# Four seams of a hybrid recurrent step: two hidden tiles' plain products first, operands in token halves, residual rows on GpSimd's DMA queue

## The chip, the cores and the metric

The kernel runs on one core of one Trainium2 chip. The metric is the device time of one execution in microseconds. Before the change three runs gave 2541.56, 2547.58 and 2551.4 us; the median is 2547.58 us.

## The reference, cut to what matters

One inference step of a two-layer trunk over 1048 columns (16 meta tokens and 1024 prompt tokens of one sequence, then 8 samples of one token each), in float32. Layer 0 is a mixer of gated linear attention and an S5 state space; layer 1 is a Griffin block (convolution, RG-LRU). After each mixer comes the same gated ConvFFN, and its two ends are what the change touches:

```
def conv_ffn(x, buf, norm, w_up, conv_w, conv_b, w_down):
    hup = rmsnorm(x, norm) @ w_up                     # 1024 -> 2 x 2816
    gate, val = jnp.split(hup, 2, axis=-1)
    gate, new_buf = causal_dwconv(gate, buf, conv_w, conv_b)   # width 3
    return x + (jax.nn.gelu(gate) * val) @ w_down, new_buf     # 2816 -> 1024

def trunk(x, ...):
    for layer in range(DEPTH):
        if layer % 2 == 0: x, ... = even_mixer(x, ...)   # x + mix @ w_out_0
        else:              x, ... = odd_mixer(x, ...)    # x + y @ w_out_1
        x, nb = conv_ffn(x, buf_ffn[layer], ...)
    return rmsnorm(x, norm_final), ...
```

## The kernel before, in words

Everything lies transposed: 128 channels on the partitions, T tokens in the free dimension (1048 columns; HALF is 524), so the residual is eight tiles X 0 to 7 of 128 x T. A float32 product is made of three fp32r matmuls (`mm3`, L123 to L130): high part by high, low by high, high by low. `split` (L84) makes the parts: a cast on ScalarE (L85) and a subtraction on VectorE (L45, the helper that records every `tensor_tensor`; L48 records the fused `scalar_tensor_tensor`). Weights come by SyncE's DMA queue in tiles of 128 x 512 (`load_w`) and are split in the same way.

The up projection (`ffn_up`) runs over 22 tiles of hidden channels (`hidden(t)`). Each needs a gate and a value for both token halves, a 2 x 2 block product in (gate, value) and (input channels) by (token halves), which is made with seven products (Strassen's scheme in Winograd's form) in the order B11, B21, T2, T3, T1, B22, T4. A product is 4 column tiles x 3 parts x 2 chunks of 262 columns, that is 24 matmuls. B11, B21 and B22 are plain: their operand is a gained half of X, their weight a block as it is. T1 to T4 have sums: of X halves on one side (`Seven.sums`, for a pair of column tiles j and j + 4, so four chains of them), of weight blocks on the other (`sums(t)` in `ffn_up`, on GpSimd, into the tiles wS from wA). All operands are split into high and low, `o[op, j]`. The output hdr[t] goes to memory.

The operands are built where the new residual comes to be. For layer 0 that is the loop after the mixer (i from 0 to 7 over X tiles, the last product of w_out0, L1027 to L1048): PE makes two products, VectorE adds them to x, ScalarE squares and GpSimd adds up the squares (`stats`, the tile acc), x is stored to xdn[m] by SyncE, the plain operand is split off, and after every second tile follow the sums. For layer 1 it is `out(*steps_[-1], prev)` with `after` (L1471 to L1479): the Griffin block runs over token halves and four groups G, and the last of these steps completes X. Its eight B11 and B21 operands are split just ahead of that call; they need only the first token half. The column sum over the partitions is a matmul with a tile of ones (`colsum`, L147) into a PSUM bank, and the inverse norm RB is made from it (`rinv_from`). It scales the products afterwards, so products can start before it is there.

At the head of `ffn_up` the convolution's cache FC is loaded on ScalarE's queue and GpSimd makes the cached terms `pre` from it. Then hidden(0) asks for its weights, the weight sums and the products in the order above.

The down projection (`ffn_down`) first loads X 0 to 7 back from xdn on SyncE's queue (L1174), then goes in turns over hidden tiles: first tiles 0 and 1, then five turns of four. For each tile of a turn hr is loaded from hdr[t] (L1180, two buffers) and split into ph and pl (six buffers each). Each of the eight output tiles then takes k x 3 matmuls a chunk of 352 columns into one of four banks and an addition to X[m]. In layer 0 the last turn also makes the operands of the Griffin block (`Next.step`: HL, X with its gain, split), in layer 1 the final norm.

The order of the work: the framework takes the instructions in the order of the program, with `tc.high_priority()` and `tc.issue_after()` moving some, and lays them out on the engines by a simulated time; on the chip each engine and each DMA queue is in order. Tiles live in pools that are opened at the left or the right end of SBUF; a tile placed where an older one lay waits for that one's last reader (`reuse_waits="tile"`), which is how a load at a seam can be held by the work of the stage before.

Of the kernel before, what the change touches and what calls it, by code (L numbers as in the profile page):

```python
# [9 lines left out]
F32 = mybir.dt.float32  # L10
# [29 lines left out]
def hybrid_step_kernel(ctx: ExitStack, tc: tile.TileContext, a: dict):  # L40
# [896 lines left out]
    NEG = cst.tile([128, 16], F32, name="NEG")  # L937
    ts(NEG, CV[:, CV_GF0:CV_GF0 + 16], -1.0, MUL)
# [5 lines left out]
    class Stats:  # L944
# [5 lines left out]
        def finish(self, before=None):  # L950

            while self.late and (before is None or self.late[0][0] <= before):
                _, c0, n = self.late.pop(0)
                rinv_from(self.acc[c0], n, RB[:, c0:c0 + n])
# [12 lines left out]

    class Next(Stats):


        def __init__(self, gain, pool):
            super().__init__()
            self.gain = gain
            self.HL = [new_hl(pool, k) for k in range(8)]

        def step(self, m, x, c0, n):
            self.n_ += 1
            self.finish(self.n_ - LATE)
            split_gain(self.HL[m][0][:, c0:c0 + n], self.HL[m][1][:, c0:c0 + n], x, self.gain + m)
# [4 lines left out]
    class Seven(Stats):  # L984


        def __init__(self, layer, pool, stats=None):
            super().__init__()
            if stats:
                self.acc, self.late, self.n_ = stats.acc, stats.late, stats.n_  # L990
            self.gain, self.ng = CV_GF0 + 8 * layer, 8 * layer
            self.o = {}
            for j in range(4):
                self.new(j, OPS if j < 3 else OPS[:2] + OPS[5:6], pool)

        def new(self, j, ops, pool):
            for k in ops:
                self.o[k, j] = tuple(pool.tile([128, HALF], F32R, name=f"{k}{j}{x}") for x in "hl")
# [6 lines left out]
        def sums(self, j, x1, x2, pool):  # L1005

            g1, g2 = (CV[:, self.gain + m:self.gain + m + 1] for m in (j, j + 4))
            n1 = NEG[:, self.ng + j:self.ng + j + 1]
# [14 lines left out]

    bms, bm = open_pool("bm0", "right")
    xts, xt = open_pool("xt0", "right")
    nx = Seven(0, bm)
    for i in range(8):  # L1027
# [11 lines left out]
        nc.sync.dma_start(out=xdn[m], in_=x)  # L1039
        nx.plain(j, x, "B21" if i % 2 else "B11")  # L1040
        if m == 7:
            l0.close()
            bls, bl = open_pool("bl0")
            nx.new(3, OPS[2:5] + OPS[6:], bl)
# [10 lines left out]
    def ffn_up(layer, nx):  # L1055
# [11 lines left out]
        wv = CV[:, CV_FC + layer * 4 * NFF:CV_FC + (layer + 1) * 4 * NFF].rearrange("p (j t) -> p j t", j=4)  # L1067

        def wb(j):
            return wv[:, j].unsqueeze(2).to_broadcast([128, NFF, 8])  # L1070

        pt = fp.tile([128, NFF, 8], F32, name="pt")
        tt(pre, FC[:, :, 0], wb(0), MUL, P)
        tt(pre, pre, wb(3), ADD, P)
        tt(pt, FC[:, :, 1], wb(1), MUL, P)
        tt(pre, pre, pt, ADD, P)
        P.tensor_copy(out=FC[:, :, 0], in_=FC[:, :, 1])
# [7 lines left out]
        def sums(t):  # L1085

            r = {}
            for i, k in ((1, 0), (1, 1), (0, 0), (0, 1)):
                r[i, k] = fp.tile([128, 512], F32, name="wA", bufs=4)
                nc.sync.dma_start(out=r[i, k], in_=block(t, i, k))  # L1090
            s1, s2, s3, s4_ = (fp.tile([128, 512], F32, name="wS", bufs=3) for _ in range(4))
# [12 lines left out]
        def hidden(t):  # L1104
            w11, w12 = plain(t, 0, 0), plain(t, 0, 1)
            ws2, ws3, ws1, ws4 = sums(t)
            w22 = plain(t, 1, 1)
            R = fp.tile([128, 2 + T], F32, name="R", tag="rvc", bufs=5)
            VL = fp.tile([128, T], F32, name="VL", tag="rvc", bufs=5)
            P.memset(R[:, 0:2], 0.0)  # L1110
            Z = [bank() for _ in range(2)]
            W, Y = ([ps.tile([128, 512], F32, name="p", tag="aux", bufs=4) for _ in range(2)] for _ in range(2))
# [561 lines left out]
```

## Time and profile before

| | |
|---|---|
| median of three runs | 2547.58 us (2541.56 to 2551.4) |
| profiled execution | 2545.16 us, span 2542.5 us |
| PE busy | 2369.5 us, 93% (17427 matmuls) |
| VectorE (DVE) busy | 1797.4 us, 71% |
| ScalarE (ACT) busy | 1116.6 us, 44% |
| GpSimd (POOL) busy | 556.5 us, 22% |

Times in the rows are microseconds from the start of the span unless marked ns. PE is TensorE's matmul, PEld its weight load; SPq is SyncE's DMA queue and ACTq ScalarE's. `out<-in` names the tiles of the program, `L128` the line of the kernel. In square brackets stands the idle time ahead of an instruction and what ended it.

The stages of this execution: layer 0's mixer to 476; the loop that completes its residual to 525; up projection to 990; down projection 1011 to 1226; the Griffin block to 1748; its last step with the operands of the second up projection to 1801; up projection to 2251; down projection and final norm 2272 to 2543. The seams are the places between them.

### The profile page before, as it was taken

To read this page: it belongs to the slowest core of one execution; us is meant where nothing else is said; L and a number is where in the kernel's file an instruction comes from. 1 tells how busy PE (TensorE), PEld (TensorE's weight loads), DVE (VectorE), ACT (ScalarE), POOL (GpSimd) and SP (SyncE) were. 2 spreads that over 40 slices of the span, in tenths; PEclk is the share of its full clock that TensorE was granted. 3 is DMA by queue.
4 is the path that set the end of the run, shared out by engine and by line. 5 is a ranking of instruction groups with operands and counts; after the bars stand their busy time and mean duration, and the time that the engine had idled before them with its cause. 6 is when DMAs were issued, how large, how long until landed. Compare 5 with 4: busy or idle time off the path is not lost. (4 is left out here: it accounts for less than half of the span.)

```text
span 2542.5 us, 45042 instructions
## 1 busy us (share of the span) xinstructions
PE 2369.5 (93%) x17427; PEld 2325.3 (91%) x17427; DVE 1797.4 (71%) x3224; ACT 1116.6 (44%) x2226; POOL 556.5 (22%) x573
## 2 busy tenths in 40 slices
PE   7879999979999996999999999997699999969998
PEld 6778988879999996999999999997699999969998
DVE  9885788887777774554688777778777777755445
ACT  5125563644444442221566555557444444432123
POOL 4330000243344430000310001112333333300003
PEclk9899999989999998999999999999799999989999
DMA  3422325543333334332123332233333333343321
GB/s 117 104 69 81 98 78 170 188 147 117 113 113 119 115 109 153 116 114 80 49 83 101 100 99 91 91 94 130 103 113 114 121 124 120 101 165 110 95 84 68
DMA packets 200701, 277.07 MB, mean 109 GB/s; under 512 B 34312, under 2 KB 114136, under 8 KB 200488
## 3 DMA queue, kind: packets, MB, share of 16 engines
q1 hardware_dynamic: 193320, 271.24, 33.2%
q10 hardware_dynamic: 7040, 2.81, 0.5%
q8 instruction: 137, 2.24, 0.4%
q14 instruction: 76, 0.62, 0.1%
q0 software_dynamic: 128, 0.15, 0.0%
HBM read 216.69 MB, written 51.43 MB: 105 GB/s over the span
## 5 line engine op out<-in xcount | busy, mean ns | idle before, releaser
L85 ACT CAST whi<-wraw 128x512 fp32r<-128x512 f32 (+2 forms) x449 | 261.6, 590 | 529.3 <-PE bank L129 400.5
L45 DVE TENSOR_TENSOR wlo<-wraw,whi 128x512 fp32r<-128x512 f32 (+2 forms) x448 | 325.7, 734 | 107.5 <-ACT whi L85 93.0
L128 PE MATMUL bank<-H,whi 128*128 128x262 f32 (+2 forms) x1248 | 381.4, 307 | 21.4 <-DVE rgg L45 11.1
L129 PE MATMUL bank<-L,whi 128*128 128x262 f32 (+2 forms) x1248 | 380.4, 306 | 6.9 <-DVE L L48 6.9
L130 PE MATMUL bank<-H,wlo 128*128 128x262 f32 (+2 forms) x1248 | 378.3, 304 | 1.6 <-DVE wlo L45 1.6
L45 DVE TENSOR_TENSOR X<-X,bank 128x352 f32<-128x352 f32 (+4 forms) x436 | 212.3, 489 | 234.0 <-PE bank L130 231.8
L128 PE MATMUL bank<-ph,whi 128*128 128x352 f32 (+1 forms) x960 | 311.4, 325 | 41.8 <-ACT ph L85 41.8
L129 PE MATMUL bank<-pl,whi 128*128 128x352 f32 (+1 forms) x960 | 312.3, 325 | 0.0
L130 PE MATMUL bank<-ph,wlo 128*128 128x352 f32 (+1 forms) x960 | 310.5, 323 | 0.0
L45 POOL TENSOR_TENSOR acc<-acc,sq 128x352 f32<-128x352 f32 (+3 forms) x105 | 115.0, 1103 | 788.9 <-ACT sq L143 786.1
L128 PEld LDWEIGHTS bank<-H,whi 128*128 128x128 f32 x1248 | 240.5, 193 | 25.4 <-DVE rgg L45 12.2
L129 PEld LDWEIGHTS bank<-L,whi 128*128 128x128 f32 x1248 | 240.1, 193 | 12.5 <-DVE L L48 11.5
L130 PEld LDWEIGHTS bank<-H,wlo 128*128 128x128 f32 x1248 | 240.3, 193 | 3.1 <-DVE wlo L45 1.9
L45 DVE TENSOR_TENSOR wlo<-wS,whi 128x512 fp32r<-128x512 f32 x176 | 123.0, 700 | 153.8 <-ACT whi L85 153.5
L85 ACT CAST whi<-wS 128x512 fp32r<-128x512 f32 x176 | 109.2, 621 | 270.1 <-PE p L129 149.7
L128 PEld LDWEIGHTS bank<-ph,whi 128*128 128x128 f32 x960 | 181.8, 189 | 42.2 <-ACT ph L85 42.2
L129 PEld LDWEIGHTS bank<-pl,whi 128*128 128x128 f32 x960 | 181.8, 189 | 1.3 <-DVE pl L45 0.5
L130 PEld LDWEIGHTS bank<-ph,wlo 128*128 128x128 f32 x960 | 182.1, 190 | 0.0
L45 POOL TENSOR_TENSOR wS<-wA 128x512 f32<-128x512 f32 x88 | 150.3, 1708 | 120.9 <-DVE wlo L45 117.6
L45 POOL TENSOR_TENSOR wS<-wA,wS 128x512 f32<-128x512 f32 x44 | 57.4, 1306 | 392.3 <-DVE wlo L45 392.3
L48 DVE SCALAR_TENSOR_TENSOR C<-R,CV,C 128x1040 f32<-128x1040 f32 x88 | 131.7, 1497 | 0.8 <-ACT C L1152 0.8
L128 PE MATMUL bank<-ryh,whi 128*128 128x262 f32 x372 | 105.7, 286 | 3.2 <-ACT ryh L85 1.8
(613 smaller groups left out, 7076.5 us busy)
## 6 DMA issues: line engine op xcount, KB each, us to landing
wA<-in_w_up SPq DMA_DIRECT2D x176, 256.0 KB, 2.7
wraw<-in_w_up SPq DMA_DIRECT2D x132, 256.0 KB, 4.9
wraw<-in_w_in SPq DMA_DIRECT2D x96, 256.0 KB, 2.6
hdr<-VL SPq DMA_DIRECT2D x44, 524.0 KB, 4.0
hr<-hdr SPq DMA_DIRECT2D x44, 524.0 KB, 3.6
wraw<-in_w_dn SPq DMA_DIRECT2D x80, 256.0 KB, 2.7
wraw<-in_w_out SPq DMA_DIRECT2D x48, 256.0 KB, 2.6
xdn<-X SPq DMA_DIRECT2D x16, 524.0 KB, 3.3
```

Source lines behind the costliest of these rows:

```text
L45: return (eng or V).tensor_tensor(out=o, in0=x, in1=y, op=op)
L48: V.scalar_tensor_tensor(out=o, in0=x, scalar=s, in1=y, op0=op0, op1=op1)
L85: A.copy(out=h, in_=x)
L128: PE.matmul(out=out, lhsT=wh, rhs=xh, start=first and i == 0, stop=False, **kw)
L129: PE.matmul(out=out, lhsT=wh, rhs=xl, start=False, stop=False, **kw)
L130: PE.matmul(out=out, lhsT=wl, rhs=xh, start=False, stop=last and i == n - 1, **kw)
```

## The change

It changes the following.

- **Plain products ahead.** `hidden` becomes a generator. For tiles 0 and 1 the two products B11 and B21 (with the addition into R) come first, of both tiles; then the column sums (`nx.finish()`), and then the rest of tile 0 and tile 1. In the rest the weight sums and, for tile 0, the load of FC (now on SyncE's queue) and the cached terms. The banks of `rinv_from` in the seams come from the other group of PSUM tiles ("aux").
- **Sums.** `Seven.sums` makes its sums with scaled copies on ScalarE and plain subtractions on GpSimd in place of fused operations on VectorE.
- **Places.** Layer 0's wA and wS get a pool of their own (fw0), opened before the operands. The operands are allocated by kind rather than by column tile, so that B11 and B21 lie together at the low end. p1 and R are asked for first in `hidden`.
- **Second up projection.** The Griffin block's operands HL are two tiles of half the tokens each (`halves`). When its first half is done, the places of the first-half tiles take B11 and B21, which are built at step G 2 of the second half; the places of the second half take T2 and T3 at the last step.
- **Residual.** The stores to xdn and the loads back are issued on GpSimd's queue. The loads of the down projection stand after the loads of hr for tiles 0 and 1.
- **Down projection.** ph and pl of tiles 2 and 3 (2 to 5 in layer 1) have fixed places that are allocated first, as has the last turn's weight pool dl in layer 1.

```diff
-    def rinv_from(acc, n, out):
-        p = bank()
+    def rinv_from(acc, n, out, tag=None):
+        p = ps.tile([128, 512], F32, name="p", tag=tag, bufs=4) if tag else bank()
...
-            self.HL = [new_hl(pool, k) for k in range(8)]
+            self.HL = [[halves(pool, half, k) for k in range(8)] for half in range(2)]
...
         def sums(self, j, x1, x2, pool):
...
-            A.activation(out=b12, in_=x1[:, HALF:], func=ACTF.Copy, scale=g1)
-            stt(t1, x1[:, :HALF], n1, b12, MUL, ADD)
-            stt(t2, x2[:, HALF:], g2, t1, MUL, SUB)
+            gained(t1, x1[:, :HALF], g1)
+            gained(b12, x1[:, HALF:], g1)
+            tt(t1, b12, t1, SUB, P)
+            gained(t2, x2[:, HALF:], g2)
+            tt(b12, t2, b12, SUB, P)
+            tt(t2, t2, t1, SUB, P)
             split(*self.o["T2", j], t2)
-            stt(b12, x2[:, HALF:], g2, b12, MUL, SUB)
             split(*self.o["T3", j], b12)
             split(*self.o["T1", j], t1)
-            stt(t2, x2[:, :HALF], g2, t2, MUL, SUB)
-            split(*self.o["T4", j], t2)
+            gained(t1, x2[:, :HALF], g2)
+            tt(t1, t1, t2, SUB, P)
+            split(*self.o["T4", j], t1)
...
+    fws, fw = open_pool("fw0", "right")
     bms, bm = open_pool("bm0", "right")
     xts, xt = open_pool("xt0", "right")
-    nx = Seven(0, bm)
+    nx = Seven(0)
+    nx.new(range(4), OPS[:2], bm)
+    nx.new(range(3), OPS[2:5], bm)
+    nx.new(range(4), OPS[5:6], bm)
+    nx.new(range(3), OPS[6:], bm)
...
-        nc.sync.dma_start(out=xdn[m], in_=x)
+        P.dma_start(out=xdn[m], in_=x)
...
-    def ffn_up(layer, nx):
+    def ffn_up(layer, nx, fw=None):
...
-        A.dma_start(out=FC, in_=a["fcache"][:, layer])
...
+        def caches():
+            nc.sync.dma_start(out=FC, in_=a["fcache"][:, layer])
...
         def hidden(t):
+            ahead = t < 2
+            p1_ = [fp.tile([128, H2], F32, name="p1", bufs=2) for _ in range(2)]
+            R = fp.tile([128, 2 + T], F32, name="R", tag="rvc", bufs=5)
             w11, w12 = plain(t, 0, 0), plain(t, 0, 1)
-            ws2, ws3, ws1, ws4 = sums(t)
-            w22 = plain(t, 1, 1)
+            if not ahead:
+                ws2, ws3, ws1, ws4 = sums(t)
+                w22 = plain(t, 1, 1)
...
             prod(W, w12, "B21")
-            nx.finish()
             put(R, 2, p1, W)
+            if ahead:
+                yield
+                ws2, ws3, ws1, ws4 = sums(t)
+                w22 = plain(t, 1, 1)
+                if t == 0:
+                    caches()
...
-        for t in range(NFF):
-            hidden(t)
+        first = [hidden(t) for t in range(2)]
+        for g in first:
+            next(g)
+        nx.finish()
+        for g in chain(first, (hidden(t) for t in range(2, NFF))):
+            next(g)
...
     def ffn_down(layer, X, nxt):
...
-        for m in range(8):
-            nc.sync.dma_start(out=X[m], in_=xdn[m])
+        def place(t):
+            return tuple(dq.tile([128, T], F32R, name=f"{x}{t % 6}") for x in ("ph", "pl"))
+        places = {t: place(t) for t in ((2, 3) if nxt else (2, 3, 4, 5))}
...
-                ph, pl = (dq.tile([128, T], F32R, name=x, bufs=6) for x in ("ph", "pl"))
+                ph, pl = places.pop(t, None) or place(t)
...
+            if t0 == 0:
+                for m in range(8):
+                    P.dma_start(out=X[m], in_=xdn[m])
...
     def after(m, c0, n):
...
-            nc.sync.dma_start(out=xdn[m], in_=X[m])
+            P.dma_start(out=xdn[m], in_=X[m])
...
+        if half and G == 2:
+            for i, op in enumerate(("B11", "B21")):
+                for j in range(4):
+                    nxt.o[op, j] = halves(hlp, 0, 4 * i + j)
+                    nxt.plain(j, X[4 * i + j], op)
...
     rqs.close()
-    hls.close()
     bms, bm = open_pool("bm1", "right")
     t7s, t7 = open_pool("t7")
-    nxt = Seven(1, bm, nxt)
-    for j in range(4):
-        nxt.plain(j, X[j], "B11")
-        nxt.plain(j, X[j + 4], "B21")
+    for i, op in enumerate(("T2", "T3")):
+        for j in range(4):
+            nxt.o[op, j] = halves(hlp, 1, 4 * i + j)
+    nxt.new(range(3), ("T1", "B22", "T4"), bm)
     out(*steps_[-1], prev)
```

## Rows read from the trace of the kernel before

**Rows 1.** Windows: stretch, length, busy PE PEld DVE ACT POOL, clock, DMA, GB/s.

```profile
476.00:525.00 49.00, 44.73 (x265) 43.84 (x266) 43.70 (x67) 29.61 (x56) 22.51 (x20) 0.95 0.45 154
...
544.00:990.00 446.00, 445.90 (x3646) 445.60 (x3646) 318.01 (x457) 193.54 (x373) 167.27 (x151) 1.00 0.34 113
990.00:1011.40 21.40, 0.42 (x5) 0.20 (x3) 4.77 (x8) 2.11 (x5) 0.00 (x0) 0.61 0.81 302
1011.40:1226.00 214.60, 214.60 (x1327) 213.83 (x1328) 116.62 (x229) 51.53 (x108) 0.00 (x0) 0.99 0.32 99
...
1748.00:1802.00 54.00, 22.00 (x166) 20.73 (x164) 48.98 (x72) 31.51 (x60) 20.13 (x23) 0.73 0.35 128
```

**Rows 2.** Timeline of PE at its restarts: start, duration, instruction, idle time before.

```profile
524.45 1.54 PE L147 MATMUL bank<-acc,ones 128*128 128x352 f32 x2 [3.72 <-POOL acc L45]
...
543.59 0.59 PE L128 MATMUL bank<-T20h,whi 128*128 128x262 f32 x1 [8.58 <-ACT whi L85]
...
1011.40 0.66 PE L128 MATMUL bank<-ph,whi 128*128 128x352 f32 x1 [20.98 <-ACT ph L85]
...
1761.61 0.29 PE L130 MATMUL bank<-ryh,wlo 128*128 128x262 f32 x1
...
1801.17 0.59 PE L128 MATMUL bank<-T20h,whi 128*128 128x262 f32 x1 [29.02 <-ACT whi L85]
...
2271.88 0.66 PE L128 MATMUL bank<-ph,whi 128*128 128x352 f32 x1 [20.77 <-ACT ph L85]
```

**Rows 3.** Timeline of SyncE's queue ahead of layer 0's down projection.

```profile
994.77 0.34 SPq L1162 DMA_DIRECT2D hdr<-VL  x1
995.16 4.63 SPq L1174 DMA_DIRECT2D X<-xdn  x8
999.98 1.98 SPq L1180 DMA_DIRECT2D hr<-hdr  x2
```

**Rows 4.** Summary of the tile X from 990 to 1012 us.

```profile
DMA to landing us min/median/max: 4.8/7.6/10.2
```

**Rows 5.** The page's DMA issues: KB each, median us to landing.

```profile
hr<-hdr SPq DMA_DIRECT2D x44, 524.0 KB, 3.6
```

**Rows 6.** Timeline of ACT at the same seam.

```profile
1010.86 1.25 ACT L85 CAST ph<-hr 128x352 fp32r<-128x352 f32 x3 [17.51 <-DMA hr<-hdr]
```

**Rows 7.** Timelines of POOL, ACT and DVE ahead of the first T2.

```profile
537.65 0.66 POOL L45 TENSOR_TENSOR pre<-FC,CV 128x176 f32<-128x176 f32 x1 [9.40 <-DMA FC<-in_fcache]
...
1793.08 0.34 ACTq L1064 DMA_DIRECT2D FC<-in_fcache  x1
...
1794.61 0.63 DVE L45 TENSOR_TENSOR T43l<-t,T43h 128x524 fp32r<-128x524 f32 x1
...
1795.28 0.49 POOL L45 TENSOR_TENSOR pre<-FC,CV 128x176 f32<-128x176 f32 x1 [14.77 <-DMA FC<-in_fcache]
...
1797.87 1.25 POOL L45 TENSOR_TENSOR wS<-wA 128x512 f32<-128x512 f32 x1
...
1800.50 0.62 ACT L85 CAST whi<-wS 128x512 fp32r<-128x512 f32 x1 [6.30 <-POOL wS L45]
```

**Rows 8.** Layer 1's seam: a group (busy, mean ns, idle), then POOL's and SyncE's timeline.

```profile
L1010 ACT ACTIVATE t<-X,CV 128x524 f32<-128x524 f32 x4 | 2.9, 728 | 0.0
...
1750.50 10.31 SPq L1475 DMA_DIRECT2D xdn<-X  x7
...
1757.64 13.74 POOL L45 TENSOR_TENSOR acc<-acc,sq 128x262 f32<-128x262 f32 x14 [57.38 <-ACT sq L143]
```

**Rows 9.** Groups of POOL by form (busy us, mean ns); the page's queue row.

```profile
L45 POOL TENSOR_TENSOR wS<-wA 128x512 f32<-128x512 f32 x88 | 150.3, 1708 | 120.9 <-DVE wlo L45 117.6
...
L45 POOL TENSOR_TENSOR s5WS<-s5WS,s5ZA 128x520 f32<-128x520 f32 x4 | 5.3, 1329 | 0.1
...
L455 POOL DMA_DIRECT2D out_o_s<-s5SO x4 | 2.8, 709 | 26.6 <-DVE s5SO L45 26.6
...
q0 software_dynamic: 128, 0.15, 0.0%
```

More of the change, by code (lines that the diff above doesn't have):

```diff
@@ L953, in finish @@
                 _, c0, n = self.late.pop(0)
-                rinv_from(self.acc[c0], n, RB[:, c0:c0 + n])
+                rinv_from(self.acc[c0], n, RB[:, c0:c0 + n], "aux")
         def stats(self, m, x, c0, n):
@@ L966, in add, with halves @@
                 self.late.append((self.n_, c0, n))
+    def halves(pool, half, k):
+        return tuple(pool.tile([128, HALF], F32R, name=f"{'ab'[half]}{k}{x}") for x in "hl")
     class Next(Stats):
@@ L978, in step @@
             self.finish(self.n_ - LATE)
-            split_gain(self.HL[m][0][:, c0:c0 + n], self.HL[m][1][:, c0:c0 + n], x, self.gain + m)
+            for half in range(2):
+                a0, a1 = max(c0, half * HALF), min(c0 + n, half * HALF + HALF)
+                if a0 < a1:
+                    s_ = slice(a0 - half * HALF, a1 - half * HALF)
+                    split_gain(*(z[:, s_] for z in self.HL[half][m]), x[:, a0 - c0:a1 - c0], self.gain + m)
             self.add(m, x, c0, n)
@@ L984, in hybrid_step_kernel, with __init__, new @@
     class Seven(Stats):
-        def __init__(self, layer, pool, stats=None):
+        def __init__(self, layer):
             super().__init__()
-            if stats:
-                self.acc, self.late, self.n_ = stats.acc, stats.late, stats.n_
-            self.gain, self.ng = CV_GF0 + 8 * layer, 8 * layer
+            self.gain = CV_GF0 + 8 * layer
             self.o = {}
-            for j in range(4):
-                self.new(j, OPS if j < 3 else OPS[:2] + OPS[5:6], pool)
-        def new(self, j, ops, pool):
+        def new(self, js, ops, pool):
             for k in ops:
-                self.o[k, j] = tuple(pool.tile([128, HALF], F32R, name=f"{k}{j}{x}") for x in "hl")
+                for j in js:
+                    self.o[k, j] = tuple(pool.tile([128, HALF], F32R, name=f"{k}{j}{x}") for x in "hl")
         def plain(self, j, x, k):
@@ L1043, in hybrid_step_kernel @@
             bls, bl = open_pool("bl0")
-            nx.new(3, OPS[2:5] + OPS[6:], bl)
+            nx.new((3,), OPS[2:5] + OPS[6:], bl)
         if i % 2:
@@ L1088, in sums @@
             for i, k in ((1, 0), (1, 1), (0, 0), (0, 1)):
-                r[i, k] = fp.tile([128, 512], F32, name="wA", bufs=4)
+                r[i, k] = (fw or fp).tile([128, 512], F32, name="wA", bufs=4)
                 nc.sync.dma_start(out=r[i, k], in_=block(t, i, k))
-            s1, s2, s3, s4_ = (fp.tile([128, 512], F32, name="wS", bufs=3) for _ in range(4))
+            s1, s2, s3, s4_ = ((fw or fp).tile([128, 512], F32, name="wS", bufs=3) for _ in range(4))
             tt(s1, r[1, 0], r[1, 1], ADD, P)
@@ L1122, in keep @@
                 for c in range(2):
-                    u = fp.tile([128, H2], F32, name=nm, bufs=2)
+                    u = p1_[c] if nm == "p1" else fp.tile([128, H2], F32, name=nm, bufs=2)
                     with tc.high_priority():
@@ L1136, in hidden @@
             prod(W, w12, "B21")
-            nx.finish()
             put(R, 2, p1, W)
+            if ahead:
[4 more added lines that the diff above has]
+                    caches()
+            VL = fp.tile([128, T], F32, name="VL", tag="rvc", bufs=5)
+            Y = [ps.tile([128, 512], F32, name="p", tag="aux", bufs=4) for _ in range(2)]
             prod(Z, ws2, "T2", False)
@@ L1172, in ffn_down @@
         es, dq = open_pool(f"dn{layer}")
-        for m in range(8):
-            nc.sync.dma_start(out=X[m], in_=xdn[m])
+        def place(t):
+            return tuple(dq.tile([128, T], F32R, name=f"{x}{t % 6}") for x in ("ph", "pl"))
+        places = {t: place(t) for t in ((2, 3) if nxt else (2, 3, 4, 5))}
+        if not nxt:
+            dl = [tuple(dq.tile([128, 512], F32R, name=f"{x}{m}") for x in ("wh", "wl")) for m in range(8)]
         for t0, k in TURNS:
@@ L1190, in ffn_down @@
             if last and not nxt:
-                ds, dl = open_pool("dl")
-                fx = ds.enter_context(tc.tile_pool(name="fx", bufs=1, reuse_waits="tile"))
+                ds, fx = open_pool("fx")
                 ws = []
-                for m in range(8):
-                    h, l = (dl.tile([128, 512], F32R, name=f"{x}{m}") for x in ("wh", "wl"))
+                for m, (h, l) in enumerate(dl):
                     load_into(h, l, block(m), 512)
@@ L1267, in final_step @@
             fdone[:] = [(c0, n, facc[-1] if end else None)]
-    ffn_up(0, nx)
+    ffn_up(0, nx, fw)
     bls.close()
     bms.close()
+    fws.close()
     hls, hlp = open_pool("hl1", "right")
@@ L1363, in xr @@
                 p = bank()
-                mm3(p[:, :n], kslices(w), cols(HL, h0 + c0, n))
+                mm3(p[:, :n], kslices(w), cols(HL[half], c0, n))
                 nx.finish(None if j else nx.n_ - 1)
@@ L1450, in gelu_branch @@
                 p = bank()
-                mm3(p[:, :n], kslices(w), cols(HL, h0 + c0, n))
+                mm3(p[:, :n], kslices(w), cols(HL[half], c0, n))
                 tt(gg[:, c0:c0 + n], p[:, :n], RB[:, h0 + c0:h0 + c0 + n], MUL)
@@ L1511, in out @@
                         after(m, h0 + c0, n)
-    nxt = Stats()
+    nxt = Seven(1)
     early = [(m, c0, n) for m in range(8) for c0, n in HCH]
@@ L1549, in hybrid_step_kernel @@
     nx = nxt
-    nx.new(3, OPS[2:5] + OPS[6:], bl)
+    nx.new((3,), ("T1", "B22", "T4"), bl)
     t7s, t7 = open_pool("t7")
@@ L1559, in hybrid_step_kernel @@
     bms.close()
+    hls.close()
     xps, xp = open_pool("xp2")
```

27 lines of the change are left out of this document (12 added, 15 removed).

## The prediction, before the result was known

> **What bounds the kernel now.** I read the windows by stage first, then TensorE's timeline where it restarts, then, backward from each restart, the queue of the engine named as its releaser. The reader should see in the windows that the two feed-forward stages have nothing to give while they run: in the first up projection PE is busy 445.9 of 446.0 us and in the down projection after it 214.6 of 214.6 us, both at the full granted clock [rows 1]. What is lost lies at the four seams. PE's timeline shows the idle time ahead of each first matmul [rows 2]: 3.72 us for the column sum and 8.58 us for the first T2 product where layer 0's up projection starts; 20.98 us where its down projection starts; 29.02 us for T2 in layer 1; 20.77 us before layer 1's down projection. That is 83 us of a profiled execution of 2545.16 us (span 2542.5). It stands 2.42 us under the median of the runs, 2547.58, and I add those at the end.
>
> Two things end these waits. Ahead of a down projection it is SP's queue in its order: the last hdr store, eight X loads in 4.63 us of issuing, and only then the two hr loads [rows 3]. Eight X of 524 KB land up to 10.2 us after their issue [rows 4], so an hr load, which takes 3.6 us in the median of the whole run [rows 5], lands at 1010.8, when ACT ends a 17.51 us wait with the first split [rows 6]; PE follows 0.5 us later. Ahead of an up projection it is the operands and then one DMA: in layer 1 DVE is busy 48.98 of 54.00 us of the seam [rows 1], the last operand's low half starts at 1794.61, the load of FC went onto ACT's queue at 1793.08 behind the casts, GpSimd waits for it until 1795.28, spends 2.6 us on the cached conv terms, and only then makes the weight sums whose cast (1800.50) PE waits for. Layer 0 has the same wait for FC at 537.65 [rows 7].
>
> **The change part by part.** Prices first. A scaled copy of 524 columns on ACT takes 0.73 us [rows 8]. A GpSimd subtraction of 524 columns isn't in the trace in that form; the nearest by size takes 1.33 us (520 columns), a 512-column one 1.25 us beside a quiet DVE [rows 7] and 1.71 us in the mean over 88, most of them beside a busy DVE [rows 9]. I take 1.4, since the new code takes four scalar_tensor_tensors a column tile off DVE; ends 1.25 and 1.71. A DMA issued by GpSimd costs it 0.71 us at 37 KB, the 0.15 MB of its queue over four [rows 9]; at 524 KB I take the same, as the number of pieces is alike (128 rows against 256 by the shapes in the code); its other end is proportional to bytes, 14 times that, and is the third rival. A product is 24 matmuls of 0.122 us (445.90 over 3646) [rows 1], 2.93 us; two plain products make 5.9.
>
> *Down seam, layer 0.* The hr loads no longer stand behind X, which goes to GpSimd's queue. Counting bytes in the pools, hr and the ph/pl of hidden tiles 0 and 1 now lie on the first places of bm0, which hold B11 and B21. The last hidden tile reads these first, and five products follow: 14.7 us in which 3.6 us of loading and the splits (1.25 us for three on ACT [rows 6]) fit. X 0 to 2 lie on T2, T3 and T1 of the last column tile, free before PE's end as well. So PE can go on; it has four banks, 24 matmuls at 0.162 us (214.60 over 1327 [rows 1]), 3.9 us, before it needs X added, and DVE is then still finishing the last hidden tile (4.77 us busy [rows 1]). I take 1.5 us of idle time, so the gain is 19.5; ends 21 (no wait at all, and no slow clock after it: the granted clock of that window is 0.61) and 12 (X lands late). Cover of the remaining X loads: the first turn takes 24 x 6 matmuls x 0.162 = 23 us, against some 1.3 us for each X, 10.2 us spread over eight [rows 4].
>
> *Down seam, layer 1.* The same, except that hr's first buffer, by the same count, begins 816 bytes below the end of bm1, whose last tile is a T4 operand, and T4 is the last product. So the first hr load waits for PE's end: 3.6 us, 0.5 for the first cast, 0.5 to PE, and some 0.5 for X 0 behind the stores of the caches: 5 us idle, gain 15.5; ends 9 and 20 (my count is off by one tile).
>
> *Up seam, layer 1.* Removed from it: the eight B11 and B21 splits on ACT and DVE (now at step G 2 of the second half, where PE has other work; I put 1 us of loss there, ends 0 and 3), 16 DVE subtractions, FC's load ahead of the sums, eight xdn stores on SP. Added: 12 more scaled copies on ACT, 16 subtractions and 8 store issues on GpSimd. GpSimd then has 14 adds (13.74 us [rows 8]), 16 x 1.4 and 8 x 0.71: 41.8 us. It can begin when the first X is stored, at 1750.50 [rows 8], and has no slack. The chain of one column tile is of like length, since three t7 buffers serve all: copy 0.73, three subtractions 4.2, three casts and a low half 2.4, copy 0.73, subtraction 1.4, and about 0.8 for nine handovers: 10.2. The first tile's last subtraction comes at some 1765.5, the fourth's at 1796. Then what is late is new: wA now lies on X 6, X 7 and the first t7 buffer, and wS on t7, because p1 and R are asked for first. The weight sums wait for the last T4 split: 1.4 us, then two sums of 1.25 and a cast of 0.62 [rows 7]: T2 at about 1801, where it was (1801.17). But both tiles' plain products are done by then, one of them new in that time: gain 5.9, I say 6. At 1.25 a subtraction the four chains end 2.4 us sooner and the slots fill better (gain up to 12); at 1.71 they end 5 us later (gain 1).
>
> *Up seam, layer 0.* GpSimd: 21 adds at 1.13 (22.51 over 20 [rows 1]) 23.7, 16 x 1.4, 8 x 0.71: 51.8 us, against 44.73 of PE in that loop [rows 1]; begun one X tile in, at about 482, it ends near 535. PE ends the loop at 520.73 (524.45 less 3.72), does the sum and four plain products in 0.8 + 11.7 us, 2.5 more at the half clock: 535.7. The weight tiles have places of their own (fw) and are loaded long before, so sums slip into GpSimd's pauses: T2 at about 537 where it was 543.6. With 5.9 us of work moved ahead that is 12.5; I take 11, as the first column sum may still hold PE, ends 1 and 15.
>
> Sum: 19.5 + 15.5 + 6 + 11 - 1 = 51; 2545.2 - 51 = 2494, and on the scale of the median 2497. The rest (half tiles of HL, the fixed ph places, aux banks for the column sums) stands beside full PE work and I cost it at nothing; without cover the 8 extra splits of the last turn would be 8 x 0.73 us of ACT.
>
> A rule of the Trainium skill speaks against the move to GpSimd: its page SBUF — State Buffer, "Who interferes with whom", says that a DVE instruction with two SBUF inputs and a GpSimd instruction that reads SBUF exclude each other for the whole instruction. The trace agrees in direction: 1.25 us against the mean 1.71 [rows 7, 9]. By it all 32 subtractions would cost the upper price and hold DVE too, which gives the first rival's time.
>
> **Rivals.** (1) GpSimd becomes the up seams' bound at the contended price. 32 x 0.4 us more than I took, all on the path: the up seams give back 13 of their 17 us, 2510. For it: the two engines slow each other; against: DVE loses most of its two-input work there. (2) The streams are put out in an order in which the early loads don't pass: hr or X stays queued behind the last tile's stores, and the down seams keep most of their 21 us. Then only the up seams' 16 and some 10 are left: 2522, or 2532 without those 10. For it: SP's queue kept such an order before [rows 3]; against: the two now have different queues. (3) Slower: a 524 KB DMA costs GpSimd's queue much more than 0.71 us. With d us each, the 16 stores add 16 x (d - 0.7) to the GpSimd-bound up seams, and the X loads lengthen a down seam by 8 x d less 24 us once that is positive. At d = 3.4 that is 43 + 6, near the whole gain; at d = 4 it is 53 + 16, hence 2565. For it: only four small DMAs of that queue are in the trace, and the price per byte is unknown; against: pieces, not bytes, are what is issued. The Trainium skill's SBUF page names a mechanism that would do it (the "DVE blocks DMA" trap: descriptors of a GpSimd DMA are not written while DVE holds the shared port); no such delay shows in the four.
>
> **How the numbers follow.** Forecast 0.62 (2478 to 2508 by its own bounds); (1) 0.14; (2) 0.12; (3) 0.08; better than all bounds 0.04. Range 2477 to 2528: it takes in (1) and the better part of (2). About 0.5%, 13 us, is what a measurement of this kernel can tell from no change; faster by that holds for the forecast, (1), most of (2) and a little of (3): 0.87; same 0.06; slower 0.07.
>
> **What would show it.** PE's idle time before the first ph product under 3 us in layer 0 and about 5 in layer 1, released by a split; hr loads issued before PE's last T4. Before the first T2 product two tiles' B11 and B21; T2 itself near the same distance from the last ryh product in layer 1 as now (39 us, 1801.17 less 1761.9 [rows 2]), and GpSimd busy over 40 us of that seam where it was 20.13 of 54. Wrong would be: T2 released by a weight sum long after the last operand, X adds that hold PE in the first turn, or DMA instructions of over 2 us on GpSimd.

## The result: faster by a third of what was forecast

The changed kernel takes 2529.29 us in the median of five runs (2526.4 to 2539.03), beside 2547.58 for the kernel before (2541.56 to 2553.25 over five runs then). The ratio is 0.9935, 95% interval 0.9908 to 0.9963: 18 us less where I had forecast 51, and 1.3 us above my range. The profiled execution has a span of 2527.4 us (time 2529.29), 15.1 less than before.

Cut where PE passes from stage to stage, the profiled executions of both kernels and of three variants (e1, e3 and e11, told of below) divide as follows, in us.

| stretch | before | after | e1 | e3 | e11 |
|---|---|---|---|---|---|
| start to the loop after layer 0's mixer | 476.1 | 474.7 | 479.6 | 477.5 | 479.9 |
| loop, seam and up projection 0 | 514.3 | 519.7 | 508.9 | 508.8 | 508.9 |
| idle ahead of down projection 0 | 21.0 | 13.1 | 12.5 | 3.4 | 3.4 |
| down projection 0 | 256.1 | 257.9 | 257.3 | 262.8 | 258.6 |
| layer 1's mixer | 494.4 | 491.4 | 496.5 | 495.4 | 492.9 |
| seam and up projection 1 | 489.2 | 487.2 | 478.6 | 478.8 | 477.0 |
| idle ahead of down projection 1 | 20.8 | 10.9 | 10.7 | 4.4 | 4.4 |
| down projection 1 | 258.1 | 260.1 | 260.8 | 260.8 | 262.2 |
| end | 12.5 | 12.5 | 12.5 | 12.3 | 12.9 |

A down projection is counted to its last product; layer 0's ends at 1267.5 us in before, and not at 1226 as the stages given ahead have it. The first stretch and that of layer 1's mixer vary by 5 us and more between kernels that are alike in them, so their 1 and 3 us prove nothing. The four seams together give 10.6 us: +5.3, -6.0, -2.0 and -7.9, a down seam taken with the projection behind it.

PE's restarts in the trace of after answer to [rows 2] (start, duration, instruction, idle time ahead; b0h is layer 1's first T2 operand, which now lies on a half-token tile):

```profile
511.98 0.43 PE L128 MATMUL bank<-H,whi 128*128 128x344 f32 x1 [2.11 <-DVE X L45]
535.66 1.54 PE L147 MATMUL p<-acc,ones 128*128 128x352 f32 x2 [5.07 <-POOL acc L45]
551.77 1.41 PE L147 MATMUL p<-acc,ones 128*128 128x352 f32 x4 [0.97 <-DVE R L45]
552.75 0.55 PE L128 MATMUL bank<-T20h,whi 128*128 128x262 f32 x1
1007.48 0.66 PE L128 MATMUL bank<-ph,whi 128*128 128x352 f32 x1 [13.14 <-ACT ph L85]
1796.43 2.09 PE L147 MATMUL p<-acc,ones 128*128 128x262 f32 x4 [27.99 <-DVE R L45]
1802.15 0.59 PE L128 MATMUL bank<-b0h,whi 128*128 128x262 f32 x1 [3.63 <-ACT whi L85]
2254.89 0.66 PE L128 MATMUL bank<-ph,whi 128*128 128x352 f32 x1 [10.90 <-ACT ph L85]
```

Two faults show in them. In layer 0's up seam the 8.58 us ahead of T2 are gone, with 0.97 left ahead of the column sum before it; but PE now waits inside the loop, where it hardly waited before: seven waits of 0.58 to 2.11 us for an X addition on DVE, 8.8 us together, and 5.07 ahead of the column sum. And the down seams have kept half of their wait.

**Why DVE is late in the loop.** The windows of the loop itself, columns as in [rows 1], for after and for e1 (sums on VectorE); then DVE's and POOL's timeline of after at one place:

```profile
474.70:530.60 55.90, 46.87 (x264) 44.32 (x264) 42.89 (x51) 32.62 (x60) 41.38 (x38) 0.95 0.46 157
```

```profile
479.64:526.74 47.10, 44.89 (x264) 43.21 (x264) 43.97 (x64) 28.30 (x54) 29.01 (x27) 0.97 0.56 188
```

```profile
507.54 3.95 DVE L48 SCALAR_TENSOR_TENSOR B221l<-X,CV,B221h 128x524 fp32r<-128x524 f32 x1 [0.84 <-ACT B221h L89]
511.41 0.51 DVE L45 TENSOR_TENSOR X<-X,bank 128x352 f32<-128x352 f32 x1
...
507.45 1.32 POOL L45 TENSOR_TENSOR t<-t,t 128x524 f32<-128x524 f32 x1
508.74 0.94 POOL L45 TENSOR_TENSOR acc<-acc,sq 128x352 f32<-128x352 f32 x1
509.65 1.28 POOL L45 TENSOR_TENSOR t<-t,t 128x524 f32<-128x524 f32 x1
```

DVE does 13 instructions fewer than in e1 in nearly the same busy time, 0.84 us each for 0.69. B221l shows how. The same instruction takes 0.75 us while GpSimd is quiet (B223l at 545.26), and B221l took 1.44 at this place in before. Here it takes 3.95, and ends at 511.49, 0.56 us after the last of three GpSimd instructions that followed one another without a pause. The X addition waits behind it in DVE's queue, and PE for that (the 2.11 above). GpSimd's own price was as I took it, 1.38 us in the mean of 32 (I took 1.4), and a 524 KB DMA costs its queue 0.57 us (groups of POOL by form: busy, mean ns, idle):

```profile
L45 POOL TENSOR_TENSOR t<-t,t 128x524 f32<-128x524 f32 x32 | 44.0, 1377 | 15.3 <-ACT t L1013 14.6 <-issue 0.4
...
L1052 POOL DMA_DIRECT2D xdn<-X x8 | 4.6, 571 | 82.3 <-DVE X L45 82.3
```

Layer 1's up seam has the same at a larger scale. DVE and POOL there:

```profile
1770.62 8.18 DVE L45 TENSOR_TENSOR T11l<-t,T11h 128x524 fp32r<-128x524 f32 x1 [3.14 <-ACT T11h L85]
...
1795.24 0.70 DVE L45 TENSOR_TENSOR T43l<-t,T43h 128x524 fp32r<-128x524 f32 x1 [2.07 <-ACT T43h L85]
...
1770.58 5.02 POOL L45 TENSOR_TENSOR t<-t,t 128x524 f32<-128x524 f32 x4
1775.57 1.42 POOL L45 TENSOR_TENSOR acc<-acc,sq 128x262 f32<-128x262 f32 x2
1776.96 1.28 POOL L45 TENSOR_TENSOR t<-t,t 128x524 f32<-128x524 f32 x1
...
1798.84 1.26 POOL L45 TENSOR_TENSOR wS<-wA 128x512 f32<-128x512 f32 x1 [4.22 <-DMA wA<-in_w_up]
```

A subtraction of 0.7 us takes 8.18, until seven GpSimd instructions in a row have ended. The last operand is done 39.1 us after the mixer's last product (1756.80), where my working had 35.5, and the weights' loads, which by my count of the pools wait for its place, put another 3 between it and the first weight sum. GpSimd isn't the bound there, as I had it: from 1750 to 1796 it is busy 35.2 of 46.0 us and waits for ScalarE's copies in between.

**Why the down seams keep their wait.** SP's and ACT's queue ahead of layer 0's down projection, in answer to [rows 3, 6]:

```profile
992.32 0.36 SPq L1197 DMA_DIRECT2D out_o_fcp<-fcp  x1
992.73 0.93 SPq L1196 DMA_DIRECT2D out_o_fcs<-FC  x1
993.77 4.17 SPq L113 DMA_DIRECT2D wraw<-in_w_dn  x2
998.71 0.34 SPq L1186 DMA_DIRECT2D hdr<-VL  x1
999.10 1.57 SPq L1216 DMA_DIRECT2D hr<-hdr  x2
...
1006.95 1.25 ACT L85 CAST ph<-hr 128x352 fp32r<-128x352 f32 x3 [9.66 <-DMA hr<-hdr]
```

X is out of that queue, as the change says. But hr still stands in it behind the last hidden tile's stores, and the last of these waits for VL until 998.71. The places were free long before: B11 and B21, on which hr lies by my count, are read for the last time at 980. The loads then land 7.8 and 10.1 us after their issue, beside eight X loads, for the 3.6 of [rows 5].

### The profile page after: what moved, and what is told of

Its sections match the earlier page's. It is cut to its first block, busy times and chain, and to the rows that moved or that the text cites. A ratio compares the mean times of both kernels' runs of the same rounds, so it can differ in the third digit from the quotient of the medians.

```text
span 2527.4 us, 45164 instructions
## 1 busy us (share of the span) xinstructions
PE 2365.9 (94%) x17427; PEld 2318.0 (92%) x17427; DVE 1811.7 (72%) x3199; ACT 1133.1 (45%) x2258; POOL 620.4 (25%) x637
## 5 line engine op out<-in xcount | busy, mean ns | idle before, releaser
L128 PEld LDWEIGHTS bank<-ph,whi 128*128 128x128 f32 x960 | 181.9, 190 | 29.9 <-ACT ph L85 25.5
L128 PE MATMUL bank<-H,whi 128*128 128x352 f32 (+1 forms) x480 | 160.8, 338 | 19.0 <-DVE X L45 9.0
L129 PE MATMUL bank<-L,whi 128*128 128x352 f32 (+1 forms) x480 | 160.2, 336 | 6.8 <-DVE L L48 6.6
L130 PE MATMUL bank<-H,wlo 128*128 128x352 f32 (+1 forms) x480 | 157.9, 331 | 0.9 <-DVE wlo L45 0.9
L128 PEld LDWEIGHTS bank<-H,whi 128*128 128x128 f32 x480 | 93.1, 195 | 23.3 <-DVE X L45 9.4
L129 PE MATMUL bank<-ryl,whi 128*128 128x262 f32 x372 | 105.6, 285 | 0.6 <-DVE ryl L45 0.6
L130 PE MATMUL bank<-ryh,wlo 128*128 128x262 f32 x372 | 105.2, 284 | 0.0
```

Of the source, the lines that this page charges most:

```text
L128: PE.matmul(out=out, lhsT=wh, rhs=xh, start=first and i == 0, stop=False, **kw)
L129: PE.matmul(out=out, lhsT=wh, rhs=xl, start=False, stop=False, **kw)
L130: PE.matmul(out=out, lhsT=wl, rhs=xh, start=False, stop=last and i == n - 1, **kw)
```

## The experiments

**e1, operand sums back on VectorE.** From after; the sums alone.

```diff
-            tt(t1, b12, t1, SUB, P)
...
+            stt(t1, x1[:, :HALF], n1, b12, MUL, ADD)
+            stt(t2, x2[:, HALF:], g2, t1, MUL, SUB)
```

> The changed kernel with the operand sums of both up projections made as before (one scaled copy on ScalarE, four fused operations on VectorE), all else as changed. Theory: GpSimd's subtractions hold up VectorE's two-input instructions (the low half of B22 took 3.95 us in the changed kernel, 0.75 alone), the additions to X queue behind them, and PE waits in layer 0's loop. Then that loop falls from 55.9 us (474.69 to 530.60) back to about 45, the first T2 product of layer 0 comes some 10 us earlier, and the run takes about 2518. Rival: the loop is slow because of the eight stores that GpSimd issues or because of the three buffers of X that wait for them; then it stays near 55 us and the time within 3 us of 2529.

2514.01 us (2510.66 to 2519.37), ratio 0.9865 (0.9846 to 0.9884). Loop and up projection 0 fall by 10.7 us, up projection 1 by 8.6. The loop itself takes 47.1 us, and the waits in it are down to one of 0.95 and four under 0.4. Ahead of the column sum 4.96 us stay (3.72 in before), so these are not the subtractions' doing; what they come from is open. In the medians the sums on GpSimd cost the changed kernel 15 us.

**e4, the same question from the other side.** From before, only the sums are moved to ScalarE and GpSimd (the lines of `sums` in the change's diff).

> The kernel before with one part of the change alone: the operand sums by scaled copies on ScalarE and subtractions on GpSimd. Theory: the loop ahead of layer 0's up projection takes some 10 us longer as in the changed kernel, and layer 1's seam does not gain as it has the same chain and the same late weight sums: 2555 to 2565. Rival (what was predicted): VectorE is relieved and both seams gain some, 2535 to 2545.

2567.0 us (2564.95 to 2570.45), ratio 1.0072 (1.0056 to 1.0088): 19 us slower by that edit alone, just above the 2555 to 2565 that I expected. Layer 0's loop to the column sum takes 56.4 us for 48.3, seam and up projection 1 502.3 for 489.2. Without the rest of the change the moved sums make the kernel slower than it was. Both edits, e1 and e4, also exchange the chain: four copies on ScalarE and four subtractions on GpSimd stand for one copy and four fused operations on DVE. In layer 0's loop the trace shows the hold itself, as PE waits for X additions behind it. In layer 1 these runs don't part the hold from the longer chain, so the hold's share there isn't shown.

**e2, hr of the first two tiles on GpSimd's queue.** From after.

```diff
-                nc.sync.dma_start(out=r, in_=hdr[t])
+                (P if t0 == 0 else nc.sync).dma_start(out=r, in_=hdr[t])
```

> The changed kernel with the hr loads of hidden tiles 0 and 1 on GpSimd's queue ahead of the X loads instead of SyncE's. Theory: they waited in SyncE's queue behind the store of the last hidden tile (issued 998.71, hr at 999.10) though their places were free since 977 to 980. On GpSimd's queue they are issued at about 992.5 and land by 997, the casts follow the last GELU at 997.3, and PE's idle time falls from 13.1 to about 4 us in layer 0 and from 11.3 to about 5 in layer 1: about 2514. Rival: the transfers themselves are the limit (ten of 524 KB together); then hr lands at 1002 or later and the gain is under 5 us in all.

2524.5 us (2522.93 to 2529.47), ratio 0.991 (0.9892 to 0.9929). The idle time ahead of the down projections falls from 13.14 to 3.37 and from 10.90 to 4.33. So most of the wait was the order of the queue. GpSimd's queue of e2, and ACT behind it:

```profile
989.89 0.34 POOL L1180 COPY fcp<-R 128x2 f32<-128x2 f32 x1 [19.73 <-DVE R L45]
990.39 0.61 POOL L1216 DMA_DIRECT2D hr<-hdr  x1
991.17 0.55 POOL L1216 DMA_DIRECT2D hr<-hdr  x1 [0.18 <-issue]
991.71 2.13 POOL L1224 DMA_DIRECT2D X<-xdn  x4
...
994.05 1.17 ACT L1183 ACTIVATE C<-C 128x524 f32<-128x524 f32 x2 [1.13 <-DVE C L48]
995.13 1.24 ACT L85 CAST ph<-hr 128x352 fp32r<-128x352 f32 x3
```

What is left in layer 0 is the last hidden tile's own work. The first hr lands at 995.09, and ACT's casts of it follow the last GELU (994.05 to 995.22) without a pause; that GELU had waited for DVE. So a still earlier load alone would gain nothing there.

The whole falls by 4.8 us only, where I expected 15 (2514); the rival's time came without its condition, as hr lands at 995 and not after 1002. Of the 9.8 us gained in layer 0, 6.1 are given back inside the down projection (264.0 us for 257.9), and 1.1 in layer 1's. Layer 1's mixer took 4.4 us more in this execution, which its spread allows.

**e3, both.** e1 and e2 together.

> The two edits together: sums on VectorE as before, and hr of tiles 0 and 1 on GpSimd's queue ahead of X. Theory: the seams are separate and the gains add, 11 and 15 us off 2529: about 2503. Rival: what one gives the other takes (slow clock or DMA after each seam): not under 2512.

2504.22 us (2501.61 to 2508.89), ratio 0.9826 (0.9809 to 0.9844); I expected 2503. In the seams of the profiled executions the two gains add up: 20.1 us in e1, 9.2 in e2, 29.9 in e3. In the medians e3 gains 5 us more than both (25.1 for 15.3 and 4.8), as much as the stretches outside the seams vary by. Where layer 0's down projection gives back, PE and DVE show:

```profile
989.65 0.43 PE L128 MATMUL bank<-ph,whi 128*128 128x352 f32 x1 [3.37 <-ACT ph L85]
1003.91 0.43 PE L128 MATMUL bank<-ph,whi 128*128 128x352 f32 x1 [4.54 <-DVE X L45]
...
1002.90 0.53 DVE L45 TENSOR_TENSOR pl<-hr,ph 128x352 fp32r<-128x352 f32 x1 [6.47 <-ACT ph L85]
1003.34 0.51 DVE L45 TENSOR_TENSOR X<-X,bank 128x352 f32<-128x352 f32 x1
```

The split of hidden tile 2, of the next turn, stands ahead of an addition to X in DVE's queue, and its load (issued 991.98) lands only at 1002.3 among the X loads. DVE waits 6.47 us for something that TensorE doesn't need yet.

**e5, without the plain products ahead.** From e3.

```diff
-            ahead = t < 2
+            ahead = False
```

(and `nx.finish()` and `caches()` called in tile 0, between B21 and the addition into R).

> The version with sums on VectorE and hr on GpSimd's queue (2504.2), with the plain products of the second hidden tile no longer ahead: tile 0 runs whole, then tile 1. Theory: in layer 1 two products (5.9 us) fell into a wait of 20 us and were a clear gain; in layer 0 the wait ahead of T2 is nearly gone, so less than that: 2504 plus 7 to 12, 2511 to 2516. Rival: the wait only moves, as the last operand sets T2 either way and tile 1's plain products are done later in time that is free: 2504 to 2507.

2513.42 us (2511.11 to 2513.85), ratio 0.9856 (0.9842 to 0.9871): 9 us more than e3 (7.6 when each is taken beside its own before), within the 2511 to 2516 expected. By stretch 3.4 in layer 0's up projection, 3.0 in layer 1's and 2.6 in its down projection. So the plain products ahead gain in both up projections, but about half of the 5.9 us each that I had priced; the 2.6 lie in a stage that they don't touch, and what they come from is open.

**e6, splits of tiles 2 to 5 behind the additions.** From e3, in both layers.

```diff
+                with ExitStack() as after:
+                    for ins in behind if t0 == 2 else ():
+                        after.enter_context(tc.issue_after(ins))
...
+                if t0 == 0 and m == 5:
+                    behind = [add.ins]
+                if t0 == 0 and m == 7 and c0 == 0:
+                    behind += [marks["ACT"].ins]
```

> The version with sums on VectorE and hr on GpSimd's queue, with the splits of hidden tiles 2 to 5 queued on VectorE and ScalarE behind the last weight of the first turn and the additions to X 5. Theory: that version gives back 6 us in the first turn of layer 0, as VectorE stands at the low half of tile 2, whose load landed at 1002.3, while additions to X wait behind it and PE for them (4.54 us at 999.38, 1.03 at 990.08; 1.11 and 1.75 in layer 1). With the order changed these go: about 2498. Rival: twelve loads of 524 KB share the DMA engines, X is late itself and the wait only moves to another addition: not under 2502.

2504.97 us (2503.71 to 2505.4), ratio 0.9824 (0.981 to 0.9839), where I expected 2498: a miss. Layer 0's down projection falls from 262.8 to 258.7 and the wait of 4.54 to 1.64. But layer 1's rises by 2.4: there the loads of tiles 2 to 5 now come too late, and PE waits 0.56 and 2.15 us for their casts between turns. In layer 0 the edit is right, in layer 1 wrong.

**e7, weights first.** From e3: wA and wS of layer 1's first hidden tile are allocated ahead of p1 and R, so that they lie on X tiles that come free early.

```diff
+            got = rooms(t) if layer and t == 0 else None
...
-                ws2, ws3, ws1, ws4 = sums(t)
+                ws2, ws3, ws1, ws4 = sums(t, got)
```

> The version with sums on VectorE and hr on GpSimd's queue, with the places of the weight sums (wA, wS) of layer 1's first hidden tile allocated ahead of p1 and R, so that they lie on X 0 to 3, which are free earlier than X 6, X 7 and the t7 buffers. Theory: the last operand is done at 1776.3 and T2 comes at 1781.7 only because the weight sums begin at 1778.3, when wA has landed; with wA there early T2 comes at about 1777: 4 to 5 us less, about 2500. Rival: R now lies on X 4 and 5 and is free later, so that the additions that empty the PSUM banks, and with them the column sums, take the place of that wait: no gain, 2503 to 2507.

2504.08 us (2502.72 to 2508.4), ratio 0.9827 (0.9811 to 0.9844): the rival's time. Seam and up projection 1 fall by 1.8 us where I expected 4 to 5, and layer 1's down projection gives 1.2 back: in its first turn PE waits 4.20 us for an X addition, where e3 has waits of 1.11 and 1.75. The loads are early, but the weight sums are not; GpSimd's queue of e7:

```profile
1772.87 0.10 POOL L1130 MEMSET R<- 128x2 f32 x1 [12.34 <-DVE T43l L45]
1773.07 1.27 POOL L45 TENSOR_TENSOR wS<-wA 128x512 f32<-128x512 f32 x1
```

They stand behind a memset of R that waits for DVE's T43l; by my count of the pools R's place is that of an X tile which DVE reads until then.

**e9, that memset on VectorE.** From e7.

```diff
-            P.memset(R[:, 0:2], 0.0)
+            V.memset(R[:, 0:2], 0.0)
```

> As e7_weights_first, and R's first two columns are set to zero by VectorE instead of GpSimd. My theory after e7: what held the weight sums of layer 1's first tile was the order of GpSimd's queue, in which they stood behind a memset of R that waits for R's place (an X tile read until 1772.06); that place is free only when VectorE is done with it, so on VectorE the memset holds nobody. GpSimd then starts these sums up to 12 us earlier (it was idle for 12.34), and the first T2 product waits for its operand alone. T2 some 4 us nearer to the end of the mixer, the second up projection's segment 473 to 474 us for 477.0, the whole 2500 (2497 to 2502). Rival: VectorE's operand splits are what T2 and T3 wait for anyway, and the wait is only passed on to the next product: 2504, as e7. Second rival: 44 more small instructions on VectorE, each held beside GpSimd's subtractions, cost more than that: over 2506.

2510.75 us (2507.44 to 2513.28), ratio 0.9846 (0.9833 to 0.986): slower than e7 by 6.7 (by 5.5 when each is taken beside its own before, 2549.42 and 2550.56), where I expected a gain of 4. The time is that of my second rival. The sums do start early. DVE of e7 first, then DVE and POOL of e9, at the same place of the program:

```profile
1766.12 2.11 DVE L48 SCALAR_TENSOR_TENSOR t<-X,CV,t 128x524 f32<-128x524 f32 x3
1768.14 0.70 DVE L45 TENSOR_TENSOR T42l<-t,T42h 128x524 fp32r<-128x524 f32 x1
...
1772.06 0.71 DVE L45 TENSOR_TENSOR T43l<-t,T43h 128x524 fp32r<-128x524 f32 x1
```

```profile
1767.22 4.12 DVE L48 SCALAR_TENSOR_TENSOR t<-X,CV,t 128x524 f32<-128x524 f32 x3
1771.26 1.77 DVE L45 TENSOR_TENSOR T42l<-t,T42h 128x524 fp32r<-128x524 f32 x1
...
1777.40 0.69 DVE L45 TENSOR_TENSOR T43l<-t,T43h 128x524 fp32r<-128x524 f32 x1
...
1767.42 1.67 POOL L45 TENSOR_TENSOR wS<-wA 128x512 f32<-128x512 f32 x1 [12.36 <-DVE t L48]
1769.17 1.61 POOL L45 TENSOR_TENSOR wS<-wS,wA 128x512 f32<-128x512 f32 x1
1770.74 1.73 POOL L45 TENSOR_TENSOR wS<-wA 128x512 f32<-128x512 f32 x1
```

From 1767.42 on GpSimd runs without a pause, DVE's instructions beside it take up to 1.77 us, and the last operands are 4.3 us later counted from the mixer's end (1744.58 in e7, 1745.65 in e9); T2 is 4.1 us later. The memset that I took for the fault had kept GpSimd out of DVE's way. The second rival's cause, 44 more small instructions on DVE, falls: they take 0.06 us each, and up projection 0, which has half of them, is at 508.9 us for 509.0 in e7. Of the 5.3 us between the profiled executions 3.8 lie in this seam and up projection and 1.3 in the two down projections.

**e10 and e11, e6's edit in layer 0 alone.** From e9 and from e7. The splits are put behind the issue of the first turn's last weight load as well.

```diff
-                    for ins in behind if t0 == 2 else ():
+                    for ins in behind if t0 == 2 and nxt else ():
```

> As e9_weights_memset, and in layer 0 alone the splits of hidden tiles 2 to 5 of the down projection are queued behind the first turn's last weight cast and the addition to X 5. In e6, where this was done in both layers, it took 4.1 us off layer 0's down projection (262.80 to 258.72) and was lost in the other seam, layer 1's down projection (+2.4) and the up projections by small amounts. My theory: the loss in layer 1 came from the same edit there, so without it layer 0's 4 us remain: 2496 if e9 is at 2500, that is 3 to 4.5 under e9. Rival: the 4 us in layer 0 were made up elsewhere by the changed order of the queues, and this run is within 1.5 of e9.

> e7_weights_first with the splits of hidden tiles 2 to 5 queued behind the first turn's last weight cast and the addition to X 5 in layer 0 alone; the memset of R is GpSimd's again. In e10 that edit was worth 4.5 us over e9, which had the same edit of the weight sums as this run's base. My theory: it is worth the same here, 2499 to 2501 against 2504.1 of e7_weights_first, layer 0's down projection at 258.5 to 259 us (263.0 there), layer 1's unchanged at 261 to 262. Rival: e10's 4.5 us lay in the spread between runs, and the whole stays at 2503 to 2505, as in e6.

e10: 2506.23 us (2501.38 to 2509.07; ratio 0.9826, 0.9813 to 0.984), 4.5 under e9. e11: 2499.98 us (2497.31 to 2503.82; ratio 0.9806, 0.9791 to 0.9821), 4.1 under e7. Layer 0's down projection is at 258.6 in both, layer 1's where it was (262.0 and 262.2). So e6's loss was in the main layer 1's own. e11 is the best version here: 29 us under the changed kernel, 49 under the one before (2549.1 beside it). It keeps a wait of 3.97 us for an X addition in layer 1's down projection.

**e8, the two engines by themselves.** No part of the step is computed: VectorE, GpSimd and ScalarE run twelve instructions of each kind, alone and side by side, all on tiles of their own.

> No part of the step: ten stretches of twelve instructions each, which measure VectorE and GpSimd by themselves and side by side on 128 x 524 (no operand shared). Theory of exclusion: VectorE with two inputs from SBUF alone takes 0.6 to 0.7 us, GpSimd alone 1.25 to 1.3; side by side VectorE's instruction waits for the end of GpSimd's, 1.3 us and more, and as GpSimd goes from one to the next, one of VectorE's can take several of these (8.18 us were seen once). A VectorE instruction with one input, or with one input from PSUM, is not held up. Rival: they share bandwidth, and both become slower by the same factor whatever VectorE reads; then every kind shows 1.2 to 1.5 us and none over 2.

The phases came out interleaved, so I read stretches. In order of time: DVE's and GpSimd's two-input subtractions side by side; DVE's alone; DVE's in the lead of a GpSimd copy; DVE's one-input form beside GpSimd; GpSimd beside DVE additions with one input in PSUM (timeline of all engines):

```profile
5.91 10.35 DVE L95 TENSOR_TENSOR ad<-dx,dy 128x524 f32<-128x524 f32 x6
7.11 8.60 POOL L107 TENSOR_TENSOR bg<-gx,gy 128x524 f32<-128x524 f32 x5
...
20.50 0.69 DVE L95 TENSOR_TENSOR cd<-dx,dy 128x524 f32<-128x524 f32 x1
...
21.88 4.38 DVE L95 TENSOR_TENSOR cd<-dx,dy 128x524 f32<-128x524 f32 x7
22.04 4.28 POOL L79 COPY bg<-bgo 128x8 f32<-128x8 f32 x1 [4.62 <-DVE bgo L77]
...
71.94 10.23 DVE L101 TENSOR_SCALAR fd<-dx 128x524 f32<-128x524 f32 x7
...
99.26 8.79 POOL L107 TENSOR_TENSOR kg<-gx,gy 128x524 f32<-128x524 f32 x7
...
104.23 3.52 DVE L104 TENSOR_TENSOR id<-dx,px 128x352 f32<-128x352 f32 x8
```

Side by side the two engines alternate: one subtraction of each takes 1.72 us (10.35 over 6, 8.60 over 5), where DVE's alone takes 0.69 and GpSimd's 1.28. With one input DVE is held as well, 1.46 us (10.23 over 7) for 0.42, which my theory had excluded. With its second input in PSUM it isn't: 0.44 us each while GpSimd is busy. And it goes both ways: beside seven DVE subtractions in a row GpSimd's copy of eight columns took 4.28 us. A long hold of DVE, as the 8.18 us in the kernel, didn't come up here: none of its instructions took over 1.86. ScalarE kept its time throughout.

## Why the prediction was right and wrong

- **What bounds the kernel** was right: what moved beyond the spread lies in the seams with the projections behind them, and e11 gains 45 us there between the profiled executions.
- **Up seam, layer 0** (11 us forecast, 5.3 lost). The failed step is that of the prices, in the words "ends 1.25 and 1.71": I bounded a subtraction by what it costs GpSimd, and it cost that. What it costs DVE stood only in the sentence on the first rival, and there I let it be 0.4 us an instruction on GpSimd. I also took it as a point against that rival that DVE "loses most of its two-input work there"; it keeps the low halves, and these were the ones that waited. e1 and e4 show the price of the moved sums: 15 us in the one kernel, 19 in the other, both up seams together. The section of the Trainium skill that I had weighed (SBUF — State Buffer, "Who interferes with whom") was the better guide; it also says: "Issue order, not op shape, decides who blocks." The trace agrees, in 3.95 us for 0.75 where GpSimd was ahead, and 4.28 for GpSimd's small copy where DVE was. It differs in the length of a hold: the Trainium skill has one instruction, and here it lasted over three and over seven.
- **Up seam, layer 1** (6 less 1 forecast, 2.0 measured). Plain products ahead were right in mechanism (e5). T2 was to come 39 us after the last mixer product, as before; it came at 45.4, since the operand chains ended 4 us late and the weights' loads took 3 more. The failed step is that GpSimd "has no slack" and sets the chains: it had slack, and what made the chains late is the 8.18 us on DVE or the handovers between the engines, which these runs don't part. The gain stays near the low end that I gave for a subtraction of 1.71, reached by another way. The 5.9 us for two products ahead were about 3 (e5).
- **Down seams** (19.5 and 15.5 forecast, 6.0 and 7.9 measured). The failed step is "So PE can go on": I counted when hr's places come free, rightly, and not what stands ahead of the load on SP's queue. That was the second rival, which I gave 0.12: hr stays behind the last tile's stores. I let some 10 us be gained under it, and 14 were. Its time, 2522, took the up seams as forecast; with the first rival's 13 us on top it is 2535, and 2529 was measured. In layer 1 the hr buffer on T4's place decided nothing, since the queue was later: PE ended at 2243.99, and hr was issued at 2249.06.
- **Cover in the first turn.** I wrote that 23 us of products cover the X loads. They do for the loads and not for DVE's queue, where the next turn's split stood ahead of an addition: 4.5 us in e3, a term that I didn't have.
- **GpSimd's DMA issue** at 524 KB costs 0.57 us for my 0.71; the third rival fell.
- **The bounds.** The ends of my parts add up to 2480 and 2528. The 2478 to 2508 that I called the forecast's own bounds is no sum of them. The measured time lies above all of them because three seams came out below their low ends: the up seam of layer 0 lost 5.3 us (low end 1 gained), and the down seams gained 6.0 and 7.9 (low ends 12 and 9).

## What to carry to other kernels

Work moved to an idle engine has a price on the engine beside it: before moving two-input work from VectorE to GpSimd, look which VectorE instruction stands in front of what TensorE waits for, and give it the longest run of GpSimd instructions without a pause as its worst case. An early load needs its place free and its queue free: follow the queue's order back to the last instruction that waits for late work. When an edit helps one stage, look for what it gives back one turn later, and apply it only where the trace shows the wait.

## What the runs showed of the hardware

GpSimd and VectorE didn't only take turns. Where one ran without a pause, the other's instruction waited for the whole run, not for one instruction: 8.18 us of DVE behind seven on GpSimd, 4.28 of GpSimd behind seven on DVE. In other stretches they alternated, 1.72 us for one of each in e8; what decides between the two isn't settled. DVE instructions with one input in PSUM went free, so here additions from TensorE's banks ran undisturbed, unless a held instruction stood in the queue ahead.
